# Transposed batched matmul, 16 x 512 x 512 x 512: output stores of two batches each, five double buffers, waits for them on the load queue, and two instruction alignments removed

## The chip, the cores and the metric

The kernel runs on one core of one Trainium2 chip. The time is device time in microseconds, the median of several executions; a profile is one of those executions. For each execution the span is listed too: the time from the first to the last instruction in the trace. The transfers that a queue (SP's or ScalarE's) has issued and that are not done yet are called its ring here; a border is a multiple of 128 slots in an engine's stream of instructions, the place to which the code's `addr_align(128)` jumps (in the profile of the kernel before, a branch at that line of VectorE at 0.97 us and of ScalarE at 0.90). A fetch, or instruction packet, is a packet of 8,192 bytes on the queue that the page calls `instruction`; whose instructions it brings the records don't say. All ratios of times in this text are the mean time of one kernel's runs over that of the kernel before in the same rounds, so they are not quite the ratios of the medians that stand beside them.

## The reference

```python
def setup_inputs():
    batch, m, k, n = 16, 512, 512, 512
    return {"a": randn(batch, k, m) as float32, "b": randn(batch, n, k) as float32}

def reference(a, b):
    return np.matmul(a.transpose(0, 2, 1), b.transpose(0, 2, 1)).astype(np.float32)
```

Each batch reads two matrices of 1 MB and writes one.

## The kernel before

SyncE (SP) issues all loads, in order, four batches deep. VectorE casts b to bf16, TensorE turns it, VectorE copies the turned b out of PSUM, ScalarE casts a, TensorE multiplies, VectorE and ScalarE each copy half of the result to an output buffer. ScalarE issues the stores of the first eleven batches, three batches late, and SP the last five once all loads are issued.

```python
LOADS = 4; OUTS = 7; LAG = 3; FETCH = 128; TAIL = 5
o_sb = [sb(f"o_sb{s}", [P, MO, N], f32) for s in range(OUTS)]
# ... (other buffers, semaphores)
def store(eng, j):
    eng.dma_start(out_v[j], o_sb[j % OUTS][:]).then_inc(
        o_out[j % OUTS] if j + OUTS < B else stored, 16)

def run_sp(sp):
    for i in range(B):
        s, use = i % LOADS, i // LOADS
        if use: sp.wait_ge(turned, i - LOADS + 1)
        sp.dma_start(b_sb[s][:], b_v[i]).then_inc(b_in[s], 16)
        if use: sp.wait_ge(summed, MO * (i - LOADS) + 1)
        sp.dma_start(a_sb[s][:], a_v[i]).then_inc(a_in[s], 16)
    for j in range(B - TAIL, B):
        # ... wait for the batch after (or, at the end, for the last copies)
        store(sp, j)

def run_dve(dve):
    # ...
    dve.addr_align(FETCH, max_nops=0)      # jump to the next border of 128 instruction slots
    cast_b(0); cast_b(1); turn(0)
    # ... the loop over batches

def run_act(act):
    act.addr_align(FETCH, max_nops=0)
    cast_a(act, 0, slice(None), 2)
    for i in range(B - 2):
        if i + 1 >= OUTS:
            act.wait_ge(o_out[(i + 1) % OUTS], 16 * ((i + 1) // OUTS))
        cast_a(act, i + 1, slice(None), 2)
        copy_out(act, i, slice(2, 4), oa_go)
        if 0 <= i - LAG < B - TAIL:
            store(act, i - LAG)
    # ... the last two batches
```

## Time and profile before

| | before |
|---|---|
| time, median (3 runs) | 125.23 us (125.19 to 125.35) |
| profiled execution: time, span | 125.51 us, 123.7 us |
| DMA engines: first data packet, last completion | 1.96 us, 122.68 us |
| bytes | 33.55 MB read, 16.78 MB written |

What SP's own queue waits for: the lines give the line of the kernel, what it waited for, the total in us, how often, and the longest wait.

```profile
SPq L93 <- PE o_ps L205: 37.7, 12, 6.0
SPq L90 <- PE bt_ps L193: 32.5, 12, 4.0
SPq L81 <- PE o_ps L205: 29.1, 4, 10.5
SPq L260 <- DMA out_dram<-o_sb: 5.8, 1, 5.8
```

Loads (L90, L93) are held up only by load buffers still in use by TensorE. No load waits for a store. The one wait for a store is the last line of the program.

The stores, in the view of the output tensor (issuing engine, number, ns to issue: least, median, most, then the first and the last issue in us):

```profile
L81 ACTq DMA_DIRECT2D out_dram<-o_sb x11: 338/338/382, 36.4 to 101.4; - x11
L81 SPq DMA_DIRECT2D out_dram<-o_sb x5: 332/332/344, 94.9 to 116.1; - x5
```

### The profile page before, as it was taken

Reading aid. Unit: us, or ns where it says so; the run is one execution under the profiler, and the core shown is the slowest. Engines: PE = TensorE matmul, PEld = TensorE weight load, DVE = VectorE, ACT = ScalarE, POOL = GpSimd, SP = SyncE. Lnnn points to the kernel's source line nnn. Section 1 sums busy time; section 2 is a strip of 40 time slices with the busy share of each in tenths; the row PEclk is TensorE's granted clock in tenths of the full one; section 3 lists DMA queues with packets and bytes.
Section 4 is the critical chain, followed back from the end, with each engine's and each line's share of the span. In section 5 each row is a group of like instructions: output and inputs, shape, how many; then the busy total and the mean of one; then the engine's idle time right before and its main releaser. Section 6 shows DMA issues by size and latency. Waiting matters only on the chain. (4 is left out here: it accounts for less than half of the span.)

```text
span 123.7 us, 1099 instructions
## 1 busy us (share of the span) xinstructions
PE 84.9 (69%) x392; PEld 48.2 (39%) x392; DVE 58.0 (47%) x50; ACT 45.9 (37%) x34; POOL 0.7 (1%) x6
## 2 busy tenths in 40 slices
PE   0042399949994997799499919919859965869600
PEld 0040155536462644455364602613535442524400
DVE  0032518455737755594653734716167370762200
ACT  0009410880466086317353080090906226034100
POOL 2000000000000000000000000000000000000000
PEclk9999999999999999999999995995899999599996
DMA  2999999999999999999999999999999999999992
GB/s 58 421 424 429 424 426 421 424 421 424 418 424 387 424 424 424 424 426 424 429 432 426 426 434 429 424 424 424 429 424 424 434 426 429 432 424 432 421 424 85
DMA packets 6914, 50.35 MB, mean 407 GB/s; under 512 B 768, under 2 KB 768, under 8 KB 768
## 3 DMA queue, kind: packets, MB, share of 16 engines
q1 hardware_dynamic: 5328, 38.80, 75.1%
q10 hardware_dynamic: 1584, 11.54, 22.1%
q14 instruction: 2, 0.02, 0.1%
HBM read 33.55 MB, written 16.78 MB: 407 GB/s over the span
## 5 line engine op out<-in xcount | busy, mean ns | idle before, releaser
L205 PE MATMUL o_ps<-bt_sb,a_bf 128*128 128x512 bf16 x256 | 67.5, 414 | 22.7 <-PEq L183 22.4
L205 PEld LDWEIGHTS o_ps<-bt_sb,a_bf 128*128 128x128 bf16 x256 | 28.5, 116 | 55.2 <-issue 33.8
L123 ACT CAST a_bf<-a_sb 128x2048 bf16<-128x2048 f32 (+1 forms) x16 | 29.6, 1847 | 33.8 <-DMA a_sb<-in_a_dram 33.8
L137 DVE CAST b_bf<-b_sb 128x2048 bf16<-128x2048 f32 x16 | 19.5, 1222 | 24.8 <-DMA b_sb<-in_b_dram 24.8
L132 DVE COPY o_sb<-o_ps 128x1024 f32<-128x1024 f32 (+1 forms) x17 | 19.7, 1160 | 20.3 <-PE o_ps L205 20.3
L193 PE MATMUL bt_ps<-identity,b_bf 128*128 128x128 f32 x136 | 21.0, 303 | 8.7 <-PEq L183 8.7
L132 ACT COPY o_sb<-o_ps 128x1024 f32<-128x1024 f32 (+1 forms) x17 | 16.3, 961 | 27.2 <-PE o_ps L205 27.2
L193 PEld LDWEIGHTS bt_ps<-identity,b_bf 128*128 128x128 f32 x136 | 20.3, 209 | 12.9 <-issue 10.9
L143 DVE COPY bt_sb<-bt_ps 128x1024 f32<-128x1024 f32 x16 | 19.5, 1221 | 11.6 <-PE bt_ps L193 11.6
L123 ACT ACT_TABLE_LOAD x1 | 1.3, 1283 | 9.1 <-DMA a_sb<-in_a_dram 9.1
L123 DVE CAST a_bf<-a_sb 128x1024 bf16<-128x1024 f32 x1 | 0.7, 694 | 0.5 <-DMA a_sb<-in_a_dram 0.5
L109 POOL TENSOR_SCALAR_AFFINE_SELECT identity<-identity 128x128 f32<-128x128 f32 x1 | 0.3, 292 | 0.2 <-POOL identity L107 0.2
L107 POOL MEMSET identity<- 128x128 f32 x1 | 0.2, 204 | 0.7 <-SPq L48 0.7
L249 POOL MEMSET const-bfloat16-1.0<- 128x1 bf16 x1 | 0.1, 101 | 0.0
L249 POOL MEMSET const-uint8-127<- 128x1 uint8 x1 | 0.1, 101 | 0.0
L249 POOL MEMSET const-float32-0.0<- 128x1 f32 x1 | 0.1, 98 | 0.2 <-issue 0.2
L249 POOL MEMSET const-float32-1.0<- 128x1 f32 x1 | 0.1, 98 | 0.0
## 6 DMA issues: line engine op xcount, KB each, us to landing
b_sb<-in_b_dram SPq DMA_DIRECT2D x16, 1024.0 KB, 16.5
a_sb<-in_a_dram SPq DMA_DIRECT2D x16, 1024.0 KB, 16.4
out_dram<-o_sb ACTq DMA_DIRECT2D x11, 1024.0 KB, 9.1
out_dram<-o_sb SPq DMA_DIRECT2D x5, 1024.0 KB, 8.4
```

What stands on the lines that cost most here:

```text
L107: pool.memset(identity[:], 0.0).then_inc(id_go, 1)
L109: pool.affine_select(out=identity[:], in_=identity[:], compare_op=mybir.AluOpType.not_equal, fill=1.0, base=0, pattern=[[-1, P]], channel_ ...
L123: copy(a_bf[i % 2][:, part, :], a_sb[s][:, part, :]).then_inc(ac_go, n)
L132: copy(o_sb[i % OUTS][:, rm, :], o_ps[h][:, p, :]).then_inc(go, 1)
L137: dve.tensor_copy(b_bf[i % 2][:], b_sb[i % LOADS][:]).then_inc(bc_go, n)
L143: dve.tensor_copy(bt_sb[i % 2][:].rearrange("p j (ni no) -> p j ni no", no=NO), bt_ps[i % 2][:].rearrange("p j no ni -> p j ni no"),).then ...
L193: last = pe.transpose(bt_ps[x][:, j, no, :], w[:, no, j, :], identity[:])
L205: last = pe.matmul(o_ps[h][:, q, :], a_r[:, rk, 2 * h + q, :], bt_h[:, rk // 2, rk % 2, :], start=(rk == 0), stop=(rk == KO - 1),)
L249: nc = _bacc.Bacc("TRN2", target_bir_lowering=False, num_devices=1)
```

## The change

It is meant to halve the number of stores and to free ScalarE of waits, so that its stream and VectorE's get short enough to do without the jumps, after which two instruction packets come in the kernel before (at 1.93 and 3.41 us). The core of the diff:

```diff
-    OUTS = 7
+    OUTS = 5
     LAG = 3
-    FETCH = 128
-    TAIL = 5
+    TAIL = 3
+    H = B // 2
-        o_sb = [sb(f"o_sb{s}", [P, MO, N], f32) for s in range(OUTS)]
+        o_sb = [sb(f"o_sb{s}", [P, 2, MO, N], f32) for s in range(OUTS)]
-            eng.dma_start(out_v[j], o_sb[j % OUTS][:]).then_inc(...)
+            eng.dma_start(
+                out_v[2 * j + part.start:2 * j + part.stop].rearrange("b p mo n -> p b mo n"),
+                o_sb[j % OUTS][:, part],
+            ).then_inc(...)
@@ run_sp
                     sp.wait_ge(summed, MO * (i - LOADS) + 1)
+                if i % 2 == 0 and i // 2 >= OUTS:
+                    sp.wait_ge(o_out[i // 2 % OUTS], 16 * (i // 2 // OUTS))
                 sp.dma_start(a_sb[s][:], a_v[i]).then_inc(a_in[s], 16)
...                                     # SP stores pairs 5 and 6, then pair 7 in two halves
@@ run_dve
-            dve.addr_align(FETCH, max_nops=0)
...
-            copy_out(dve, B - 1, 0, last_go)
-            copy_out(dve, B - 1, 2, last_go)
+            copy_out(dve, B - 1, slice(0, 2), last_go)
@@ run_act
-            act.addr_align(FETCH, max_nops=0)
             cast_a(act, 0, slice(None), 2)
             for i in range(B - 2):
-                if i + 1 >= OUTS:
-                    act.wait_ge(o_out[(i + 1) % OUTS], 16 * ((i + 1) // OUTS))
                 cast_a(act, i + 1, slice(None), 2)
                 copy_out(act, i, slice(2, 4), oa_go)
-                if 0 <= i - LAG < B - TAIL:
-                    store(act, i - LAG)
+                j, odd = divmod(i - LAG, 2)
+                if odd and 0 <= j < H - TAIL:
+                    store(act, j)
...
-            copy_out(act, B - 1, 1, last_go)
+            copy_out(act, B - 1, 2, last_go)
             copy_out(act, B - 1, 3, last_go)
```

More of the change, by code (lines that the diff above doesn't have):

```diff
@@ L38 @@
     LOADS = 4
-    OUTS = 7
+    OUTS = 5
     LAG = 3
-    FETCH = 128
-    TAIL = 5
+    TAIL = 3
+    H = B // 2
+    STORED = H - (H - OUTS) + 1
     stored = tc.alloc_semaphore("stored")
@@ L77, with store @@
         oa_go = sem("oa_go")
-        def store(eng, j):
-            eng.dma_start(out_v[j], o_sb[j % OUTS][:]).then_inc(
-                o_out[j % OUTS] if j + OUTS < B else stored, 16
-            )
+        def store(eng, j, part=slice(0, 2)):
+            eng.dma_start(
+                out_v[2 * j + part.start:2 * j + part.stop].rearrange("b p mo n -> p b mo n"),
+                o_sb[j % OUTS][:, part],
+            ).then_inc(o_out[j % OUTS] if j + OUTS < H else stored, 16)
         def run_sp(sp):
@@ L92, in run_sp @@
                     sp.wait_ge(summed, MO * (i - LOADS) + 1)
+                if i % 2 == 0 and i // 2 >= OUTS:
+                    sp.wait_ge(o_out[i // 2 % OUTS], 16 * (i // 2 // OUTS))
                 sp.dma_start(a_sb[s][:], a_v[i]).then_inc(a_in[s], 16)
-            for j in range(B - TAIL, B):
-                if j + 1 < B:
-                    sp.wait_ge(summed, MO * (j + 1) + 3)
-                else:
-                    sp.wait_ge(last_go, MO)
-                store(sp, j)
-            sp.reg_mov(all_stored, 16 * OUTS)
+            for j in range(H - TAIL, H - 1):
+                sp.wait_ge(summed, MO * (2 * j + 2) + 3)
+                store(sp, j)
+            sp.wait_ge(summed, MO * (B - 1) + 3)
+            store(sp, H - 1, slice(0, 1))
+            sp.wait_ge(last_go, 3)
+            store(sp, H - 1, slice(1, 2))
+            sp.reg_mov(all_stored, 16 * STORED)
         def run_pool(pool):
@@ L131, in copy_out @@
             p = rm - 2 * h if isinstance(rm, int) else slice(None)
-            copy(o_sb[i % OUTS][:, rm, :], o_ps[h][:, p, :]).then_inc(go, 1)
+            copy(o_sb[i // 2 % OUTS][:, i % 2, rm, :], o_ps[h][:, p, :]).then_inc(go, 1)
         def run_dve(dve):
@@ L159, in run_dve @@
             cast_a(dve, B - 1, slice(KO // 2, KO), 1)
-            copy_out(dve, B - 1, 0, last_go)
-            copy_out(dve, B - 1, 2, last_go)
+            copy_out(dve, B - 1, slice(0, 2), last_go)
         def run_act(act):
-            act.addr_align(FETCH, max_nops=0)
             cast_a(act, 0, slice(None), 2)
             for i in range(B - 2):
-                if i + 1 >= OUTS:
-                    act.wait_ge(o_out[(i + 1) % OUTS], 16 * ((i + 1) // OUTS))
                 cast_a(act, i + 1, slice(None), 2)
                 copy_out(act, i, slice(2, 4), oa_go)
-                if 0 <= i - LAG < B - TAIL:
-                    store(act, i - LAG)
-            act.wait_ge(o_out[(B - 1) % OUTS], 16 * ((B - 1) // OUTS))
+                j, odd = divmod(i - LAG, 2)
+                if odd and 0 <= j < H - TAIL:
+                    store(act, j)
             cast_a(act, B - 1, slice(0, KO // 2), 1)
             copy_out(act, B - 2, slice(2, 4), oa_go)
-            copy_out(act, B - 1, 1, last_go)
+            copy_out(act, B - 1, 2, last_go)
             copy_out(act, B - 1, 3, last_go)
```

## The prediction

> **What bounds the kernel now.** I read the page from the busy shares downwards, then the DMA row, then the waits, then both ends of the run, and last the single DMA packet records behind the DMA view. The busy shares show no compute engine near its limit:
>
> ```profile
> PE 84.9 (69%) x392; PEld 48.2 (39%) x392; DVE 58.0 (47%) x50; ACT 45.9 (37%) x34; POOL 0.7 (1%) x6
> ```
>
> The slices of the page and its queues show what is:
>
> ```profile
> DMA  2999999999999999999999999999999999999992
> GB/s 58 421 424 429 424 426 421 424 421 424 418 424 387 424 424 424 424 426 424 429 432 426 426 434 429 424 424 424 429 424 424 434 426 429 432 424 432 421 424 85
> DMA packets 6914, 50.35 MB, mean 407 GB/s; under 512 B 768, under 2 KB 768, under 8 KB 768
> ...
> q1 hardware_dynamic: 5328, 38.80, 75.1%
> q10 hardware_dynamic: 1584, 11.54, 22.1%
> q14 instruction: 2, 0.02, 0.1%
> HBM read 33.55 MB, written 16.78 MB: 407 GB/s over the span
> ```
>
> The reader is to see 9s in every slice but the first and the last, at about 424 GB/s. All the traffic is needed: 33.55 MB in, 16.78 MB out. In the packet records nearly every data packet is 8,192 bytes in 309 ns, and an engine starts one every 306 ns. Each of the 16 engines carries 6,144 / 16 = 384 of them, so 384 x 306 = 117.5 us, plus 48 completion packets of 9 ns: 117.9 us. The records run from 1.96 to 122.21 us, that is 120.2 us. All that is open to any change is the difference, some 2.3 us, and 1.96 us of start and 1.5 us of end around it.
>
> The waits say the same from the other side:
>
> ```profile
> ACT a_bf L123 <- DMA a_sb<-in_a_dram: 33.8, 8, 6.4
> ACT o_sb L132 <- PE o_ps L205: 27.2, 11, 5.4
> DVE b_bf L137 <- DMA b_sb<-in_b_dram: 24.8, 7, 6.6
> ```
>
> The compute engines wait for loads; no wait for a store to free an output buffer stands in this list. The chain of work that ended last covers only 4% of the span, all PE, so I don't use it here: the end is the last store.
>
> The start and the end, from the timeline:
>
> ```profile
> 1.86 1.55 SPq L90 DMA_DIRECT2D b_sb<-in_b_dram  x1
> ...
> 6.60 1.23 DVE L137 CAST b_bf<-b_sb 128x2048 bf16<-128x2048 f32 x1 [6.60 <-DMA b_sb<-in_b_dram]
> ...
> 36.42 0.38 ACTq L81 DMA_DIRECT2D out_dram<-o_sb  x1
> ...
> 109.35 7.05 SPq L81 DMA_DIRECT2D out_dram<-o_sb  x3
> ...
> 115.46 0.58 ACT L132 COPY o_sb<-o_ps 128x512 f32<-128x512 f32 x1 [1.24 <-PE o_ps L205]
> ```
>
> The last store is issued at 116.07, but the DMA engines are busy to 122.2: there are 6.1 us of stores still in the rings. A 1 MB store alone takes 8 packets per engine, 8 x 0.306 = 2.45 us, so the last one's data can't begin before 119.75 and its issue has 3.7 us to spare. Tail compute is hidden.
>
> The first cast at 6.60 is odd. The first load's 8 packets per engine should end near 3.1 + 7 x 0.306 = 5.2. The packet records explain it. Queue 14 (instructions) has two packets of 8,192 bytes, at 1.93 (1,356 ns) and at 3.41 (309 ns). Fifteen engines start their first data packet between 1.96 and 2.81 and end it by 3.38; one starts at 3.71, just where the second instruction packet ends, and ends it at 4.55. 4.55 + 7 x 0.306 = 6.69 is about when the cast begins. So both fetches sat on one engine ahead of its data and made it 1.2 to 1.7 us late. [...] it stays late: 4.55 + 383 x 0.306 + 48 x 0.006 (a 9 ns completion packet, 3 ns of it overlapped) = 122.03. The final completion packets of the 16 engines end between 120.97 and 121.49 for fourteen of them, at 121.97 for one and 122.21 for the last. I take the last for the late one; the records don't name engines, so this is inferred.
>
> [...] loads and stores together stay at 424 whether one queue is active or two. So moving a wait or a store between ACT and SP gives no bandwidth. [...] The trace has a branch at the alignment line of VectorE (0.97 us) and of ScalarE (0.90), and two 8 KiB packets a microsecond later. One per branch in blocks of 128 slots would fit[...].
>
> **The change part by part.**
> *The alignment of VectorE and ScalarE goes.* Both branches go. The instruction counts fall (ScalarE has 70 records now, and loses a branch and 6 stores; VectorE 60, and loses a branch and a copy), [...] both instruction packets vanish, the late engine starts with the others, and the end moves from 122.21 to the next engine's, 121.97 (0.24 us) or, if that one's delay doesn't recur, to 121.49 (0.72 us).
> *Stores of 2 MB.* 16 stores become 7 of 2 MB and 2 of 1 MB: 7 completion packets fewer per engine, 7 x 9 ns = 0.06 us. The pieces stay 8 KB. ScalarE issues 5 stores instead of 11, 338 ns of its queue each, and none of it on the path.
> *Later stores.* The first store goes out after batch 4 and not after batch 3: from 36.4 to about 43.8, where the second one is now. In the loads-only stretch from 18 to 36 us packets averaged 313 to 314 ns against 309 later: 7.4 us more of it costs 7.4 x 4/309 = 0.10 us, an estimate.
> *Waits on the load queue.* SP now waits before loading a of batch 10, 12, 14 for the store of a pair. Pair 0 is issued at 43.8; sharing the engines evenly with loads, its 2 MB take 2 x 2 x 2.47 = 9.9 us and land at 53.7; that load is issued at 51.4 now. So SP stalls some 2 us. By 53.7 about 18.4 loads have drained: 16.4 by 43.8 ((43.8 - 2.9) / 2.49), then 9.9 / 4.94 = 2. 21 are issued, so 2.6 loads, 6.4 us at full rate, are still in the ring. The stall is hidden. For batch 12 it is 65 against 62.7 with 4 loads in hand; for batch 14 76.3 against 75.5 with 5.
> *Tail.* Ten batches instead of eleven are stored by ScalarE, so the loads end 2.5 us earlier (110.2 to about 107.7), and SP's queue holds 6 MB, not 5. The merged VectorE copy and ScalarE's two still end near 116, with over 3 us to spare.
> Sum: -0.24 to -0.72, -0.06, +0.10: -0.2 to -0.7 us; the middle is -0.45.
>
> **Rivals.** (1) The fetches stay: some block border lies within the streams after all, and a sequential fetch replaces the jump. Nothing in the profile tells where in a block the streams begin. For it speaks that the kernel had the alignment at all; against it, the shorter streams. Then only 0.04 us are left: 125.2. I give it a quarter. (2) The waits on SP or the burst of a 2 MB store starve the load ring: a new gap. Against it the backlog of 2.6 to 5 loads; for it, that the estimate for batch 10 leaves only 6.4 us. One gap of 2 us would give 126.8. (3) The large stores pay by themselves, through fewer fixed costs: with 9 ns each in the trace there is nothing to win, but if the transition seen at the first store (packets up to 616 ns at 38 to 42 us, 387 GB/s in that slice, some 0.35 us lost) were per store, it would be. Later stores show none, so I don't count it. (4) The tail becomes bound by compute: the last store's 3.7 us would have to go first.
>
> **Range and chances.** 125.23 - 0.45 = 124.78, and a quarter of the weight on 125.2 makes 124.85; I say 124.8. The low end, 124.3, is the full 0.72 with a little from a shorter transition; the high end, 125.3, is no fetch saved and 0.1 us lost in the longer loads-only stretch. Two per cent is 2.5 us, more than all that stands between the 117.9 us of packets and the 120.2 they take, so faster by 2% gets 0.02. Slower by 2% needs a gap of 2.5 us in a DMA row that has none: 0.04.
>
> **What would show it.** Right: no instruction packets on queue 14 in the span, the first VectorE cast near 5.3 us instead of 6.60, DMA slices still 9 throughout, the final completion packets within about 0.5 us of each other, 656 small packets on q1 and q10 instead of 768, loads done near 107.7, and no new wait that empties the loads. Wrong: queue 14 still with two packets or a stall of VectorE or ScalarE in mid-run; a slice below 9 between 50 and 80 us after an SP wait for a store; a last store issued after 119; or data packets longer than 309 ns in the 2 MB stores.

The sum came to -0.2 to -0.7 us with -0.45 in the middle. Of what it rests on, these are measured: one queue alone moves 424 GB/s (6 to 36 us) or 430 (110 to 120 us), both together 427 (60 to 110 us); from its first to its last packet the first store in the kernel before shares the engines with 133 packets of loads to its own 128, in the changed kernel 246 to 256; the latest engine in the kernel before is 0.90 us behind the median one in the first load and 0.93 in the last store. That streams with fewer instructions would need no packet inside the span was an estimate; after the change there is none, where there were two.

## The result

| | before | after |
|---|---|---|
| time, median (4 runs each) | 125.21 us (125.14 to 125.35) | 125.15 us (125.00 to 125.33) |
| ratio, 95% interval | | 0.9994 (0.9977 to 1.0011) |
| profiled execution: time, span | 125.51, 123.7 | 125.33, 123.4 |
| last completion of a store | 122.68 | 122.37 |
| instruction packets of 8 KB inside the span | 2 | 0 |

The time is the same. It lies in the range that was given. But the forecast was a gain of 0.45 us, and 0.06 us was measured, with an interval from 0.29 us gained to 0.14 us lost (0.9977 and 1.0011 of 125.2).

The page of the changed kernel, the slices of the DMA engines and the queues:

```profile
DMA  3999999999999999999999999999999999999991
GB/s 64 425 425 433 425 425 425 419 422 425 425 422 420 422 422 419 427 425 425 427 425 427 425 425 425 427 433 430 435 427 422 427 425 430 427 425 425 425 425 80
DMA packets 6800, 50.33 MB, mean 408 GB/s; under 512 B 656, under 2 KB 656, under 8 KB 656
...
q1 hardware_dynamic: 5440, 39.85, 77.4%
q10 hardware_dynamic: 1360, 10.49, 20.1%
```

Again 9s in every slice but the ends. The queue of instructions is gone and the small packets are 656 as forecast. The dip of 387 GB/s in the kernel before has no counterpart.

The start, from the timeline of VectorE, with the first cast 0.81 us earlier than the 6.60 of before:

```profile
5.79 1.23 DVE L143 CAST b_bf<-b_sb 128x2048 bf16<-128x2048 f32 x1 [5.79 <-DMA b_sb<-in_b_dram]
```

SP's own waits and the stores:

```profile
SPq L83 <- PE o_ps L203: 28.8, 3, 12.6
SPq L98 <- DMA out_dram<-o_sb: 26.7, 3, 9.0
SPq L93 <- PE bt_ps L191: 20.2, 9, 4.1
SPq L99 <- PE o_ps L203: 19.6, 7, 6.0
SPq L258 <- DMA out_dram<-o_sb: 9.4, 1, 9.4
```

```profile
L83 ACTq DMA_DIRECT2D out_dram<-o_sb x5: 378/378/417, 42.4 to 95.2; - x5
L83 SPq DMA_DIRECT2D out_dram<-o_sb x4: 344/367/399, 93.5 to 112.1; - x4
```

L98 is new: three waits of SP for a store, up to 9.0 us long. In return SP waits less for TensorE (L93 and L99). The last store is issued at 112.1 instead of 116.1, and the rings hold almost 10 us of stores when compute is done. The first store moved from 36.4 to 42.4.

So most of what the prediction wanted to see is there. What is missing is the gain, and final completions within about 0.5 us of each other: the latest is 0.96 us behind the median. To see why, one needs to look at the 16 DMA engines one by one. The trace lists when each of the 16 increments of a load's or store's semaphore lands: 768 for the 48 DMAs of the kernel before, 656 for the 41 of the changed one. Taken in order, those of the last store come 0.32 to 0.47 us after the ends of the last 16 completion packets in the kernel before, and 0.32 to 0.46 us in the changed one. So I read them as one per engine, and their spread as how far apart the 16 engines are; the trace doesn't name the engines. I take the fourth load of b, which lands near 20.5 us, and the last store. "Latest" and "second" are the latest and second latest engine, in us behind the median one.

| profile | at 20.5 us: latest, second | last store: latest, second | last completion |
|---|---|---|---|
| before | 0.92, 0.49 | 0.93, 0.55 | 122.68 |
| after | 0.20, 0.19 | 0.96, 0.08 | 122.37 |

Two engines, not one as I had inferred, start late in the kernel before, and they are gone in the changed kernel. At the end the changed kernel has one late engine all the same, as late as the worst one of before. In the kernel before no such third engine can be seen: its third latest is only 0.08 us behind at the end (0.19 in the second profile of it).

### The profile page after: what moved, and what is told of

It reads as the page before. It is cut to its first block, busy times and chain, and to the rows that moved or that the text cites. A ratio compares the mean times of both kernels' runs of the same rounds, so it can differ in the third digit from the quotient of the medians.

```text
span 123.4 us, 1091 instructions
## 1 busy us (share of the span) xinstructions
PE 81.2 (66%) x392; PEld 46.8 (38%) x392; DVE 57.9 (47%) x49; ACT 45.9 (37%) x34; POOL 0.7 (1%) x6
## 5 line engine op out<-in xcount | busy, mean ns | idle before, releaser
L203 PE MATMUL o_ps<-bt_sb,a_bf 128*128 128x512 bf16 x256 | 65.0, 403 | 21.7 <-PEq L181 21.3
L138 DVE COPY o_sb<-o_ps 128x1024 f32<-128x1024 f32 x16 | 19.6, 1225 | 20.9 <-PE o_ps L203 20.9
L191 PE MATMUL bt_ps<-identity,b_bf 128*128 128x128 f32 x136 | 19.9, 291 | 9.5 <-PEq L181 9.5
L191 PEld LDWEIGHTS bt_ps<-identity,b_bf 128*128 128x128 f32 x136 | 19.2, 207 | 12.5 <-issue 10.6
```

The costliest lines, as they stand in the source:

```text
L138: copy(o_sb[i // 2 % OUTS][:, i % 2, rm, :], o_ps[h][:, p, :]).then_inc(go, 1)
L191: last = pe.transpose(bt_ps[x][:, j, no, :], w[:, no, j, :], identity[:])
L203: last = pe.matmul(o_ps[h][:, q, :], a_r[:, rk, 2 * h + q, :], bt_h[:, rk // 2, rk % 2, :], start=(rk == 0), stop=(rk == KO - 1),)
```

## The experiments

Theory A: the fetches held up the end, and the gain is real but small. Theory B: the fetches delay engines, but another engine falls behind later by as much, and only the latest engine counts. Theory C: no effect at all. The twelve runs were made in three groups of four; each group has its own eleven executions of the kernel before (medians 125.32, 125.31 and 125.30 us).

### The parts of the change, one by one

**The changed kernel again** (no edit).

> The changed kernel once more, timed in five rounds, to get the size of the difference and to see whether the late engine at its end (0.97 us behind the median engine in the last store's completions) comes back. Theory A (the fetches held up the end, the gain is real but small): 0.2 to 0.4 us faster than before, no instruction packet in the span. Theory B (another engine falls behind among the mixed loads and stores and takes the place of the one that the fetches delayed): at most 0.3 us faster, all engines within 0.25 us of each other until the first store, and again one engine 0.6 to 1.0 us behind at the end. Theory C (no effect): ratio 1.000 within 0.001.

Measured: 125.28 us, ratio 0.9997 (0.9983 to 1.0011). No engine more than 0.2 us behind the median at 20.5 us, one 0.76 us behind at the end, last completion 122.39. That is B's picture. A's 0.2 to 0.4 us is not there. By the time alone C would fit too; what sets B apart from it are the late engines at the start and the runs with more jumps below.

**The kernel before without its alignments.**

```diff
-            dve.addr_align(FETCH, max_nops=0)
-            act.addr_align(FETCH, max_nops=0)
```

> The kernel before without its two alignments, nothing else. If ScalarE's and VectorE's longer streams cross a block border, one or two instruction packets come in mid-run, with a stall of that engine, and the time is that of before or up to 0.5 us more. If they don't cross, no packet comes in the span, the first cast starts near 5.8 us, and by theory A the time falls by 0.3 to 0.5 us; by theory B by 0.3 us at most, with a new late engine at the end.

Measured: 125.48 us, ratio 1.0014 (0.9998 to 1.0030). No packet at the start and no engine more than 0.15 us behind at 20.5 us, but one 0.86 us behind at the end, last completion 122.58. Instruction packets do come without a jump, which I read as a stream crossing a border: one at 113.8 us, and another after the end of the span. The profile's queue line has the first of them:

```profile
q14 instruction: 1, 0.01, 0.0%
```

**The changed kernel with the alignments put back.**

```diff
+            dve.addr_align(128, max_nops=0)
             cast_b(0)
...
+            act.addr_align(128, max_nops=0)
             cast_a(act, 0, slice(None), 2)
```

> The changed kernel with the two alignments put back: the store part alone. Both theories: two instruction packets near 2 and 3.4 us, one engine some 0.9 us late up to the first store, first cast near 6.6 us. Theory A: 0.0 to 0.2 us slower than before (the fetches are back and the stores start later). Theory B: the same as before within 0.15 us. If it is 0.3 us or more slower, the large late stores cost more than I estimated (0.04 us net).

Measured: 125.22 us, ratio 0.9997 (0.9982 to 1.0012). The two packets and the two late engines are back (0.91 and 0.57 us at 20.5 us):

```profile
q14 instruction: 2, 0.02, 0.1%
```

The last completion is 122.38, the same as without them. At the end there are now two engines more than 0.9 us late (0.97 and 0.91) where the changed kernel has one. This is the clearest single profile for B: the fetches come back and the end doesn't move. It shows B for the changed kernel. For the kernel before only the run without alignments speaks: there a late engine (0.86) comes in place of the two that the jumps had delayed, but why it isn't seen beside them in the kernel before is open.

**2 MB stores as two of 1 MB.**

```diff
-            eng.dma_start(<2 MB>).then_inc(...)
+            for q in range(part.start, part.stop):
+                eng.dma_start(out_v[2 * j + q], o_sb[j % OUTS][:, q]).then_inc(...)
...                                              # and the counts waited for
```

> The changed kernel with each 2 MB store issued as two 1 MB stores back to back; schedule, buffers and waits stay. 7 more completion packets per engine of 9 ns: 0.06 us slower than the changed kernel by my sum, not to be seen in the time. If it is 0.2 us or more slower, the size of a store matters by itself; if it is faster, 2 MB in one piece harms. ScalarE's stream grows by 5 instructions and may cross a block border: an instruction packet then comes in mid-run.

Measured: 125.38 us, ratio 1.0001 (0.9985 to 1.0016), last completion 122.42. No effect of a store's size, 1 MB or 2 MB, shows here. With ScalarE's five more instructions an instruction packet comes at 116.0 us, as was expected if its stream crosses a border; that the packet is ScalarE's is not shown.

**The kernel before, unchanged, as a control.**

> The kernel before, unchanged, as a control: how far its profile and its times scatter, since the first profile of it fell on an execution of 125.51 us, 0.28 above its median. Theory B (the engines that the fetches delay and the one that falls behind at the stores are different ones, and the later sets the end): fetch-delayed engines 0.5 and 0.9 us behind the median at the start, the last completion 122.4 to 122.7 us. Ratio 1.000 within 0.001. If the last completion is 122.4 or less, the 0.3 us by which the two first profiles differ are scatter and the change is worth nothing at all.

Measured: 125.34 us, ratio 1.0006 (0.9993 to 1.0020). Late engines 0.87 and 0.55 us at 20.5 us, 0.87 and 0.51 at the end, last completion 122.57. The span of the 33 other executions of the kernel before runs from 123.3 to 123.8, so the first profile of before, at 123.7, was on the slow side: a part of the 0.3 us between the two first profiles is scatter.

### What the spans say, and a cost outside them

Each execution's time and span are known, so their difference is too. Over the first group's runs, with means of all executions:

| kernel | runs | mean span | time minus span | mean time |
|---|---|---|---|---|
| before | 11 | 123.49 | 1.80 | 125.29 |
| changed | 6 | 123.37 | 1.90 | 125.26 |
| changed, aligned | 5 | 123.46 | 1.78 | 125.24 |
| before, not aligned | 6 | 123.52 | 1.98 | 125.49 |

In the profiled executions it is sharper. All six profiles of kernels with the jumps have 1.77 or 1.78 us outside the span. All seven profiles of the changed kernel and its variants without them have 1.90 or 1.91, and the kernel before without them has 2.04. The instruction packets match: six of the seven have one 8 KB packet about 1.03 us after their last instruction (at 124.45 in the changed kernel), the 1 MB variant has its one at 116.0, and the kernel before without jumps has two, at 113.8 and 125.5. So in the profiled executions each late instruction packet goes with 0.13 us more outside the span. What is shown is that putting the jumps back into the changed kernel takes 0.12 us away there, and the match over 14 profiles; that the late packets cause it is not shown. In four of the six executions of the kernel before without alignments the difference was 2.02 to 2.14 and in two it was 1.73 and 1.75, as with jumps, so there it is not the same each time.

This is one place where the gain went: without the jumps the span is 0.09 us shorter (123.46 to 123.37, which is about the scatter; a single span is on record to 0.1 us only), and the time outside it is 0.12 us longer.

### Does a delayed engine set the end at all?

If B is right, a delay larger than that of the other late engine must move the end. I made the jumps longer, by jumping to the next border twice and three times with one semaphore increment between.

```diff
+            for _ in range(3):                  # 2 in the other run
+                dve.addr_align(128, max_nops=0)
+                dve.sem_inc(pad, 1)
             cast_b(0)
...                                              # the same on ScalarE
```

> The changed kernel with three jumps to block borders on VectorE and on ScalarE ahead of their work, so up to six instruction packets at the start instead of none. Theory B: they add up on the engines that carry them, which fall 1.2 us or more behind from the start and then are the last at the end too, later than the 0.97 us of the other late engine: the end moves by 0.3 to 1 us. Rival (a late engine catches up, or the end is not set by the latest engine): no change of the end. If the packets spread over six engines at 0.3 us each, no engine passes 0.97 us and the end stays.

> The changed kernel with two jumps on each of VectorE and ScalarE, between the one that changed nothing (last completion 122.38 as without) and the three that moved the end by 1.66 us. If the latest of two late engines sets the end, the fetch-delayed engine is 1.5 to 1.9 us behind the median by 13 us, passes the slow engine's 0.97, and ends 1.3 to 1.8 behind: last completion 122.8 to 123.2, time 0.4 to 0.9 us above the changed kernel. If the end moved in the three-jump kernel because the later start of compute mattered, the time rises by a third to a half of its 1.7 us, without a late engine at the end.

| jumps on each engine | packets | at 20.5 us: latest, second | at the end: latest, second | last completion | time, ratio |
|---|---|---|---|---|---|
| 0 (changed, again) | 0 | 0.19, 0.07 | 0.76, 0.22 | 122.39 | 125.28, 0.9997 |
| 1 | 2 | 0.91, 0.57 | 0.97, 0.91 | 122.38 | 125.22, 0.9997 |
| 2 | 4 | 2.05, 1.37 | 1.86, 1.29 | 123.19 | 125.97, 1.0049 (1.0036 to 1.0061) |
| 3 | 6 | 2.78, 2.42 | 2.40, 2.08 | 124.03 | 126.99, 1.0145 (1.0126 to 1.0164) |

The queue of the run with three jumps, and its DMA slices:

```profile
DMA  3999999999999999999999999999999999999970
...
q14 instruction: 6, 0.05, 0.1%
```

The last slices, 7 and 0, are the reading: most engines are done and the two late ones still work. A delay from the start lasts for 100 us and more (2.78 us at 20.5 us, 2.40 at the end with three jumps) and comes out at the end where it exceeds the 0.8 to 1.0 us of the other late engine. In the changed kernel one of 0.97 us at the end cost nothing (last completion 122.38 against 122.39), and one of 1.86 us moved the last completion by 0.80 us. The rival, that the later start of compute did it, falls. With two jumps the first cast starts when it does in the kernel before (6.60), and yet the time is up:

```profile
6.62 1.23 DVE L144 CAST b_bf<-b_sb 128x2048 bf16<-128x2048 f32 x1 [6.62 <-DMA b_sb<-in_b_dram]
```

With three jumps it starts at 10.33 us, but the last store is issued by 115.8 and the DMA row has no gap.

Each further jump made its engine 0.7 to 1.1 us later although the packet took only 0.31 to 0.39 us, so here a further fetch cost its engine some two to three and a half times its own length. In the kernel before, the data packet after the second fetch took 838 ns instead of 309.

### Who is the other late engine?

The trace doesn't name the engines. Following the packets of the last engine back through the records does not settle it either: where engines run in step, several packets fit. With links of 2 to 5 ns between packets, the time of the data packets above 309 ns between 60 and 112 us adds up to anything from 0 to 0.40 us on the last engine's path in the changed kernel, and to as much as 0.51 us on paths of other engines.

The completions show when it falls behind. In the changed kernel the latest engine is 0.21 us behind at 40.3 us, with the next at 0.20. At 79.7, 92.0 and 96.9 us one engine alone is 0.49, 0.63 and 0.67 us behind, the next 0.09, 0.10 and 0.14. At 111.6 us it is 0.92, and from 116.5 us to the end it stays at 0.96 to 0.99. So an engine seems to fall behind little by little after the first store and to stop when loads and compute are over. Whether the mix of loads and stores, compute or something else does it is not shown.

### The waits on the load queue

**Four double buffers instead of five.**

```diff
-    OUTS = 5
+    OUTS = 4
```

> The changed kernel with four double buffers instead of five: the load queue waits for a store before batch 8, 10, 12, 14, and the first of these waits begins near 39 us, when the first store is not yet issued (43) and takes some 10 us. If the waits on the load queue are hidden by loads in hand only as long as there are some, the load ring runs dry here: loads pause for several us, a slice or two of the DMA row fall below 9 or the store has the engines alone, and the time rises by 1 to 4 us. If the time stays within 0.2 us, the waits are harmless whatever their length, because the order of loads and stores doesn't matter.

Measured: 130.16 us, ratio 1.0397 (1.0373 to 1.0421), a little above the forecast 1 to 4 us. SP's longest wait for a store is 22.5 us, and the load ring runs dry:

```profile
SPq L98 <- DMA out_dram<-o_sb: 54.6, 4, 22.5
```

```profile
DMA  3999999999999995899999999999999999999994
GB/s 69 429 413 431 429 419 426 429 411 424 434 416 413 429 431 241 282 370 372 426 429 426 429 429 424 426 426 424 424 429 429 403 372 419 311 419 439 424 429 172
```

The slices of 5 and 8, with 241 and 282 GB/s, begin at 47.9 us (15 slices of 3.19 us); in the packets the first engine stops at 49.6 and the last is back at 52.2; each loses 2.0 us on average, and all 16 together stand still for 1.5 us. With five buffers the same wait ends at 56.5 us. By then 19 loads have landed of 21 issued, and the twenty-first lands at 62.6 on the median engine, so the ring had 6 us in hand. The wait was harmless because of that and not by nature: with one buffer less the time is 4.8 us longer.

### The time of the stores

**Stores one batch after the pair**, run twice, **two batches after**, and **the kernel before with its stores one batch later**.

```diff
-    LAG = 3
+    LAG = 1        # 2 in the second; in the kernel before 4, with TAIL = 6
```

> The changed kernel with its stores one batch after the pair and not three: the first store near 30 us instead of 43. Theory of the loads-only stretch (packets of 313 ns until the first store, 309 after): some 13 us less of it, 13 x 4/309 = 0.17 us less per engine. Rival: the loss belongs to the time from 16 to 36 us or to the first stores as such; then nothing changes, and the loss at the first store only moves.

> The run with stores one batch after the pair once more, because its times fell on two levels (125.2 to 125.6 and 126.1 to 126.3) and its profile caught the lower one. If the level above comes from the loss at the first store, a profile on it shows 1.5 us or more lost per engine between 30 and 42 us; if from late engines or a gap near the end, the loss is there. If it falls on the lower level again, nothing is added but the share of the levels.

> The changed kernel with its stores two batches after the pair: the first store at about 36 us as in the kernel before, between the 43 of the changed kernel and the 31 of the run that was 0.5% slower. If an earlier first store loses more, the loss at the first store is 0.3 to 0.7 us per engine and the time 0.1 to 0.5 us above the changed kernel, perhaps with two levels of times as there. If one batch's lag was a special case (a store issued in the middle of the loads' steady stretch), this one is the same as the changed kernel within 0.15 us.

> The kernel before with its 1 MB stores one batch later (and six instead of five left to the load queue): the first store at about 43.8 us as in the changed kernel, nothing else. If the time of the first store is what made the loss at the first store smaller in the changed kernel (0.1 to 0.3 us per engine against 0.3 to 0.45), the same fall comes here: mean last completion 121.4 to 121.55 instead of 121.74, time 0.1 to 0.25 us below before. If the size of the stores did it, the loss stays at 0.3 to 0.45 and the time is that of before.

For each profile I worked out how much time per engine was lost between 16 and 50 us, where the loads-only stretch and the first store lie: 34 us, less the data packets in it times 306 ns and the small ones times 6 ns, over 16 engines. A packet counts if its middle lies in the stretch; other ways of counting at the edges move single values by up to 0.1.

| kernel | first store issued | lost per engine, 16 to 50 us | time, ratio |
|---|---|---|---|
| changed, stores one batch after (two runs) | 31.2, 31.6 | 0.94, 0.77 | 125.86, 1.0048 (1.0020 to 1.0075); 125.82, 1.0021 (0.9988 to 1.0054) |
| changed, two batches after | 35.6 | 0.55 | 125.58, 1.0015 (0.9999 to 1.0031) |
| before (two profiles); not aligned | 36.4, 36.8; 35.5 | 0.61, 0.55; 0.78 | |
| changed (two profiles), aligned, 1 MB | 42.3 to 43.5 | 0.49, 0.63, 0.45, 0.38 | |
| before, one batch later | 43.9 | 0.55 | 125.23, 0.9993 (0.9978 to 1.0009) |

My estimate that an earlier first store would save time was wrong. The packets do fall from 313 to 309 ns once stores run, but more is lost around the first store where it comes earliest. (Around it single packets took up to 616 ns in the kernel before and 606 in the changed one, and its first packet came 3.6 and 3.5 us after its issue.) The values of neighbouring rows overlap; only 0.94, in one of the two runs at 31 us, stands clear of the others. Moving the stores of the kernel before alone gave the last completion (122.38) and the time of the changed kernel, which would fit that the time of the stores, not their size, is what shortened the span. But its loss of 0.55 is that of the kernel before (0.61, 0.55), where I had expected a fall, so this stays open.

The two levels of times with the early stores have another cause. The repeated run's profile fell on the upper level (126.27 us):

```profile
DMA  2999999999999999999999999999999999987994
GB/s 47 424 437 440 424 422 422 424 419 424 419 356 424 432 430 432 427 424 427 424 430 427 432 427 424 427 427 424 432 430 427 424 427 422 427 356 314 422 416 198
```

The slices of 8 and 7 near the end are a gap: engine after engine stops from 111.3 us, the last is back at 112.9, and each loses 1.3 us on average (all 16 together stand still for 0.64 us). The run with two batches has the same from 111.1 us, 0.8 us on average. ScalarE's last store is issued at 84.4 and 87.7 us here, in the changed kernel at 95.2. With more stores done early the loads, by my estimate, end later. The last batches are computed later: SP's second store, which waits for TensorE, is issued at 111.88 and 111.26 us instead of 105.40. So, as I read it, the rings are empty before the last stores can be issued. The dip of 356 in the twelfth slice is the first store. In these two profiles no engine ends more than 0.1 us behind the median: the latest was 0.66 and 0.56 us behind before the gap and 0.12 and 0.11 after it. I had expected a loss at the first store or a gap near the end for the upper level; it is the latter.

## Why the prediction was right or wrong

**The bound: right.** All profiles with five or more buffers and the stores late enough have the DMA engines busy from 2 us to the end. That alone kept the time within the range, whose high end allowed for no gain; the gain that its middle stood for did not come.

**"Both fetches sat on one engine": wrong.** The completions show two late engines in each of the four kernels with one jump each, 0.87 to 0.92 us and 0.49 to 0.63 us behind at 20.5 us. The start and end times of packets say so too, though I had read them as one engine: a data packet starts at 3.282, just where the first instruction packet ends (3.285), and the second instruction packet starts at 3.405, just where a data packet ends (3.408). So the packet at 3.71 was not the first of its engine.

**The alignment term, "0.24 us or 0.72 us": the step that failed.** It took the next engine's end, 121.97 or 121.49, from a trace in which the others seemed ready to end there. But in the changed kernel another engine's lag of 0.8 to 1.0 us takes its place. With the jumps put back the last completion is the same (122.38 and 122.37); over six and five executions the span is 0.09 us shorter without them. And 0.12 us come on outside the span, where the prediction did not look: one instruction packet still comes, at 124.45 us, after the last instruction. Its first rival, that the fetches stay in some other form, was right in that part, though not inside the span.

**Completion packets, 0.06 us:** the count is right (656), and the run with 1 MB stores shows no difference that could be told from scatter.

**Later stores, +0.10 us: not seen.** The longer stretch of 313 ns packets is there, and stores moved still earlier did not gain what this reckoning gives them. The span of the changed kernel with alignments, 123.46, against 123.49 of before leaves the whole of the store part near nothing.

**Waits on the load queue: right, with sizes off.** The wait before batch 10 ended at 56.5 and not at 53.7 us, since the first store's first packet came 3.5 us after its issue; the loads in hand covered it. The run with four buffers shows the rival that was named.

**Tail: right, with sizes off.** The last load lands at 106.3 and not at 107.7, the last copy ends at 112.1 and not near 116, and the last store is issued with nearly 10 us in hand. The two runs with earlier stores show the rival named there.

Sum, as far as it is measured: 0.12 us less inside the span (123.49 to 123.37) and 0.10 to 0.13 us more outside it. In the changed kernel the expected gain was hidden behind another late engine, and what the span gained came back after the last instruction.

None of the runs beats both kernels. The changed kernel with alignments has the lowest mean time of its group, 125.24 against 125.26 and 125.29, which is within the scatter.

## What to carry to other kernels

In these kernels, where each transfer has 16 increments and the rings held work up to the end, the latest engine set the end, and a delay of one engine counted only where it was the largest: 0.97 us moved nothing, 1.86 and 2.40 us moved the last completion from 122.39 to 123.19 and 124.03. So look at the spread of the 16 completions of the last store before crediting the removal of one delay. Compare the time with the span too, because a cost can move from inside to outside, as about 0.1 us did here. And a wait on a queue was as harmless here as the work already in its ring: five buffers left 6 us, and four buffers cost 4%.
